# Hybrid decoder block on one core: the store of the rotary queries split over two stages, and the third stage's second scores set ahead of its gating matmuls

## The chip, the core and the metric

The kernel runs on one core of a Trainium2 chip. The metric is the device time of one execution in microseconds (us); lower is better. Inputs and output are float32 arrays in DRAM and are part of the measured program. TensorE (PE in the profile) does the matrix products, VectorE (DVE), ScalarE (ACT) and GpSimd (POOL) do the element work, and SyncE (SP) issues every DMA, in one queue and in a fixed order.

## The reference

One decoder layer of width 1024 over 528 positions (16 learned meta tokens ahead of 512 real ones). One projection feeds two attention branches of 16 heads each, MLA (latent queries and keys with a rotary part of 32) and FoX (a forget gate in the logits), both gated and merged:

```python
u = rmsnorm(h, pre_norm_g[l])
proj = u @ w_in[l]
(cq, ckv, k_pe_raw, z_mla, fq, fk, fv, f_logit, z_fox, gate_a, gate_b) = jnp.split(proj, split_idx, axis=-1)
...
q_m = jnp.concatenate([q_nope, rope(q_pe, pos)], axis=-1)
k_m = jnp.concatenate([k_nope, jnp.broadcast_to(k_pe, (B, MLA_HEADS, L, MLA_ROPE_DIM))], axis=-1)
o_mla = causal_block_attention(q_m, k_m, v_mla, MLA_SCALE)
y_mla = (o_mla * jax.nn.silu(z_mla)) @ w_br_mla[l]
...
o_fox = causal_block_attention(fox_heads(fq), fox_heads(fk), fox_heads(fv), FOX_SCALE, cum)
y_fox = (o_fox * jax.nn.silu(z_fox)) @ w_br_fox[l]
mixed = (jax.nn.sigmoid(gate_a) * y_mla + jax.nn.sigmoid(gate_b) * y_fox) @ w_out[l]
h = h + rmsnorm(mixed, post_norm_g[l])
```

The four query blocks of 128 positions see the meta tokens and the causal keys. The output leaves the meta tokens out.

## The kernel before, in words

Every product in float32 precision is made of three matmuls on a high and a low part of both operands (`wh`, `wl` of weights, `uTh`, `uTl` of the normed input). Weights arrive by DMA as `wraw` (512 KB for a block of 128 columns); ACT casts the high part (`wh`, line 130 or 604) and POOL or DVE subtracts to get the low part (`wl`, line 103).

After a first part (norms, small projections) the attention runs in 16 stages. The list `stages` has, for each of eight pairs of heads, FoX (`br` = 1) and then MLA (`br` = 0); the loop's counter `si` is 0 for the first stage. So the second stage is MLA of pair 0, the third FoX of pair 1, the fourth MLA of pair 1. In the loop, PE's order is written out by hand, as the kernel's functions are called:

- `s0()` and `s1()` are the scores: matmuls into `st`, then for each query block DVE's masked pass with the row minimum (`sf`, `nb`, line 789) and ACT's exponential (line 797). `s0` covers query blocks 0 to 2, `s1` block 3.
- `n0()` and `n1()` norm them: DVE takes reciprocals of the row sums (`su`, `ri`, lines 805 and 806), POOL does the meta columns, ACT writes the high half of the probabilities (`pn`, line 824) and DVE the low half (line 825). A DMA transpose for each of eight (block, head) pairs then turns `pn` into `pt`, one `pt` for each of the two heads.
- `va()` of a stage is its values step: matmuls `ov` of `vp` (the values, turned by a DMA transpose of `vh`) and `pt`; then DVE's gated result `gT` (line 845). It is called in the next stage, after that one's `s0`. So the third stage's PE order holds the second stage's `ov`.
- `fill` is the list of projection steps that stand between these: of a FoX stage the two gating products `z` (24 matmuls each for both branches of this pair), and the next stage's queries `mq`, keys `mk` and values `v`; of an MLA stage the next FoX stage's `fq`, `fk`, `v`. `early` says how many of its steps go between `s0` and `va`.

```python
early = {0: 3, 2: 4, 9: 4}.get(si, 0)
s0()
run(fill[:early])
for fn in late:
    fn()
s1()
```

Projection results share three PSUM buffers (`accp`), so the fourth product in a row waits until the first has been read: in the third stage `mk` waits for the reader of `z`, which is DVE's `sil` (line 738) after ACT's tanh (line 737). The instructions of DVE, ACT, POOL and SP are put in order by the framework's scheduler; PE alone follows the order of the calls, and SP where `written[0]` is set (below).

The rotary part of MLA's queries is computed before the stages for heads 0 to 7 (`pe_unit(0)`): its halves lie in rows 4 and 5 of `gT0` and `gT1`, 16 partitions for a head. Heads 0 and 1 go straight into `QP`; the six others are stored to `qpe_dram` and read back as `QP`, two heads at a time, for pairs 1 to 3. The store is four DMAs, one for each half `x` and part `i`; it is called with a range of heads:

```python
def store(x, a, b):
    for i in range(2):
        dma(qpe_dram[8 * g + a : 8 * g + b, i, x], results(x)[16 * a : 16 * b, i])
```

While `written[0]` is set, a DMA keeps its place in the order of the program on SP's queue.

Of the kernel before, what the change touches and what calls it, by code (L numbers as in the profile page):

```python
# [54 lines left out]
def block_kernel(ctx: ExitStack, tc: tile.TileContext, x, meta_tokens, pre_norm_g, w_in, fox_forget_b,  # L55
# [29 lines left out]
    written, sums_out = [False], []  # L85
# [135 lines left out]
    def run(steps):  # L221
        for _, fn in steps:
            fn()
# [324 lines left out]
    def gate_unit():  # L548

        i, br = gates.pop(0)  # L550

        def done(_, ps):
            ths[i, br] = thp.tile([128, S], F32, tag="th", name=f"th{i}{br}")
            nc.scalar.activation(ths[i, br], ps, AF.Tanh, scale=0.5)
        return unit(f"pg{i}{br}", win_w((O_GA, O_GB)[br], i), u_act, KD, REAL, done)


    with ExitStack() as att:
# [294 lines left out]

        stages = [(br, pr) for pr in range(NH // 2) for br in (1, 0)]

        vts = {}

        def feed(br, pr):
# [12 lines left out]
        pe0, rest0, store0 = pe_unit(0)  # L871
# [5 lines left out]
        for si, (br, pr) in enumerate(stages):  # L877
# [3 lines left out]
            if br == 1:  # L881

                za, zb = z_unit(1, pr), z_unit(0, pr)
                fill = (vts[br, pr] if pr else begun) + za + q + zb[:3] + k + zb[3:5] + v + zb[5:]
            elif not last:

                fill = vts[br, pr] + q + k[:KD] + v + k[KD:]
            else:
                g = gate_unit()
                fill = vts[br, pr] + g + gate_unit() + gate_unit()  # L890
# [20 lines left out]
        for si, (br, pr) in enumerate(stages):  # L911
            s0, s1, n0, n1, va = attention(br, pr)

            fill = fills[si]
            early = {0: 3, 2: 4, 9: 4}.get(si, 0)
            s0()
            run(fill[:early])
            for fn in late:
                fn()
            s1()  # L920

            if si == 0:

                run(fill[early:5])
                run(vts[1, 0] + pe_rest)
                n0()
                low[0] = nc.vector
                for ahead_ in [fn.prep for _, fn in fill[5:] if hasattr(fn, "prep")][:2]:
                    ahead_()
                low[0] = nc.gpsimd  # L930
                n1()
                first_t.extend(through)
                run(fill[5:])
            else:
                if si == 1:

                    written[0] = True
                    for x in range(2):
                        store0(x, 2, 8)
                    written[0] = False  # L940
                run(fill[early:5])
                if si == 1:

                    behind[:] = exps[:1]
                if si == 2:
                    behind.clear()
                n0()
                run(fill[5:11])
                if br:

                    behind[:] = [halved[("k", 1, pr), 1]]
                run(fill[11:12])
                if br:
                    behind.clear()
                n1()
                if 6 <= si < 8:

                    written[0] = True
                    rest1(si - 6)
                    written[0] = False  # L960
                run(fill[12:])
            written[0] = False
            if si == 1:

                behind[:] = [halved[("k", 1, 1), 0]]
            late = [va]
# [232 lines left out]
```

## Time and profile before

| what | value |
|---|---|
| median of 3 runs | 607.18 us (605.46 to 607.64) |
| profiled execution, its own time | 606.9 us |
| its span in the profile | 605.1 us |
| PE busy | 593.5 us, 98% of the span |
| second stage on PE (from its first `st`) | 80.0 to 103.2 us |
| third stage | 103.2 to 127.7 us |
| fourth stage | 127.7 to 150.7 us |

Times in a view are microseconds from the start of the span. A timeline row has start, duration, engine, line, operation, tiles, shape and count, and in brackets the idle time of the engine just before it with what ended it. "SPq" rows are DMA issues: their duration is that of the issue, not of the transfer. Matmul rows overlap by their pipeline: from start to start is the pace. PEclk is the clock that TensorE was granted, 1.00 being full.

### The profile page before, as it was taken

What the parts mean: (1) busy time and instruction counts of PE and PEld (TensorE: products, weight loads), DVE (VectorE), ACT (ScalarE), POOL (GpSimd) and SP (SyncE); (2) the same over time, 40 slices, a digit from 0 to 9 for tenths busy, and PEclk for the clock granted to TensorE, in tenths of its full rate; (3) what the DMA queues carried; (4) which work ended last, traced back from release to release, by engine and by line L of the source; (5) the groups of instructions that cost most, each with busy time, mean ns of one, the idle gap of its engine ahead of it and who ended that gap; (6) DMA issues with size and microseconds to landing.
All of it is one profiled execution on the core that took longest, in us unless ns stands there. A gap on an engine that the chain in (4) does not pass through costs nothing.

```text
span 605.1 us, 11002 instructions
## 1 busy us (share of the span) xinstructions
PE 593.5 (98%) x3777; PEld 502.9 (83%) x3777; DVE 375.2 (62%) x1004; ACT 342.4 (57%) x786; POOL 179.5 (30%) x239
## 2 busy tenths in 40 slices
PE   8999999899999999999999999999999999999996
PEld 6889889679889889889888898887888888888884
DVE  6946776564774774675766657773733624367857
ACT  7846773764773774675766748761221433243653
POOL 4317543353437544345433534530000000000000
PEclk9999999989999999999999999999999999999999
DMA  8533798988698698979797985988534323332603
GB/s 288 120 86 95 122 186 195 211 168 192 120 195 164 145 210 161 197 169 203 128 179 173 160 187 140 199 168 260 192 105 104 99 79 102 104 98 89 233 0 140
DMA packets 219960, 93.25 MB, mean 154 GB/s; under 512 B 133420, under 2 KB 211636, under 8 KB 219904
## 3 DMA queue, kind: packets, MB, share of 16 engines
q1 hardware_dynamic: 219904, 92.55, 66.3%
q8 instruction: 30, 0.49, 0.3%
q14 instruction: 26, 0.21, 0.1%
HBM read 58.10 MB, written 4.00 MB: 103 GB/s over the span
## 4 chain that ended last, share of the span: by engine, by line
PE 79%; ACT 1%; DVE 0%; issue 0%; DVEq 0%; ACTq 0%
PE py L97 14%; PE z L97 14%; PE pg L97 14%; PE st L97 7%; PE v L97 7%; PE fk L97 6%; PE fq L97 6%; PE ov L97 5%; PE x L97 4%; PE mq L97 1%; PE mk L97 1%; PE y L97 1%; PE ppe L97 0%; ACT wh L130 0%; DVE yo L1107 0%
## 5 line engine op out<-in xcount | busy, mean ns | idle before, releaser
L103 POOL TENSOR_TENSOR wl<-wraw,wh 128x1024 fp32r<-128x1024 f32 (+2 forms) x62 | 119.7, 1939 | 106.8 <-ACT wh L130 80.2
L130 ACT CAST wh<-wraw 128x1024 fp32r<-128x1024 f32 (+1 forms) x80 | 83.1, 1042 | 119.4 <-PE pg L97 38.5
L797 ACT ACTIVATE sf<-sf,nb 128x144 f32<-128x144 f32 (+3 forms) x128 | 72.0, 564 | 12.3 <-DVE nb L789 11.8
L825 DVE SCALAR_TENSOR_TENSOR pn<-sf,ri,pn 128x128 f16<-128x128 f32 (+3 forms) x128 | 69.1, 578 | 13.6 <-ACT pn L824 12.7
L824 ACT ACTIVATE pn<-sf,ri 128x128 f16<-128x128 f32 (+3 forms) x128 | 61.5, 551 | 19.5 <-ACT sf L797 16.8
L103 DVE TENSOR_TENSOR wl<-wraw,wh 128x1024 fp32r<-128x1024 f32 x34 | 41.6, 1222 | 42.8 <-ACT wh L130 42.8
L97 PE MATMUL z<-uTh,wh 128*128 128x512 f32 x128 | 51.5, 402 | 0.0
L789 DVE CUSTOM_DVE_ANT_0 sf<-st,maskt 128x272 f32<-128x272 f32 (+2 forms) x128 | 48.6, 435 | 3.9 <-PE st L97 3.9
L97 PE MATMUL z<-uTl,wh 128*128 128x512 f32 x128 | 50.5, 395 | 0.0
L97 PE MATMUL z<-uTh,wl 128*128 128x512 f32 x128 | 50.4, 394 | 0.0
L97 PE MATMUL pg<-uTh,wh 128*128 128x512 f32 x128 | 50.3, 393 | 0.0
L97 PE MATMUL pg<-uTl,wh 128*128 128x512 f32 x128 | 49.8, 389 | 0.0
L97 PE MATMUL pg<-uTh,wl 128*128 128x512 f32 x128 | 49.8, 389 | 0.0
L97 PE MATMUL py<-gh,wh 128*128 128x512 f32 x128 | 49.8, 389 | 0.0
L97 PE MATMUL py<-gl,wh 128*128 128x512 f32 x128 | 49.8, 389 | 0.0
L97 PE MATMUL py<-gh,wl 128*128 128x512 f32 x128 | 49.8, 389 | 0.0
L97 PE MATMUL st<-hlk,hlq 64*128 64x272 f32 (+3 forms) x480 | 47.3, 306 | 0.0
L97 PEld LDWEIGHTS st<-hlk,hlq 64*128 64x128 f32 x480 | 35.0, 185 | 5.8 <-ACT vh L721 2.8
L702 DVE TENSOR_REDUCE vsc<-v 128x1 f32<-128x272 f32 (+1 forms) x32 | 13.2, 432 | 38.8 <-PE v L97 38.8
L97 PE MATMUL v<-uTh,wl 128*128 128x256 f32 (+1 forms) x128 | 36.5, 285 | 0.0
L97 PE MATMUL fk<-uTl,wh 128*128 128x256 f32 (+1 forms) x128 | 36.4, 285 | 0.0
L97 PE MATMUL fk<-uTh,wh 128*128 128x256 f32 (+1 forms) x128 | 36.4, 285 | 0.0
(233 smaller groups left out, 1434.1 us busy)
## 6 DMA issues: line engine op xcount, KB each, us to landing
wraw<-in_w_in_dram SPq DMA_DIRECT2D x56, 512.0 KB
wraw<-in_w_br_fox_dram SPq DMA_DIRECT2D x8, 512.0 KB
tb<-in_w_out_dram SPq DMA_DIRECT2D x8, 512.0 KB
wraw<-in_w_br_mla_dram SPq DMA_DIRECT2D x8, 512.0 KB
wraw<-in_w_out_dram SPq DMA_DIRECT2D x6, 512.0 KB
pt<-pn SPq DMA_TRANSPOSE x128
xr<-in_x_dram SPq DMA_DIRECT2D x4, 512.0 KB
out_dram<-yo SPq DMA_DIRECT2D x8, 256.0 KB
```

Of the source, the lines that this page charges most:

```text
L97: nc.tensor.matmul(*a, **k)
L103: return eng.tensor_tensor(out=lo, in0=src, in1=f32(hi), op=ALU.subtract)
L130: nc.scalar.copy(wh[:, :n], raw[:, :n])
L702: nc.vector.tensor_reduce(out=sc[:, i : i + 1], in_=ps, op=ALU.max, axis=AX.X, apply_absolute_value=True)
L789: nc.vector.tensor_tensor_reduce(out=sf_of(h, b)[:, c0 : c0 + w], in0=ps[h][:, o : o + w], in1=maskt[:, m0 : m0 + w], scale=-scale, scalar ...
L797: exps[g] = nc.scalar.activation(sf, sf, AF.Exp, bias=sums["nb"][:, h, b : b + 1], scale=-1.0, accum_out=sums["su"][:, h, b : b + 1]).ins
L824: nc.scalar.activation(hi, sf, AF.Copy, scale=rib)
L825: nc.vector.scalar_tensor_tensor(out=lo, in0=sf, scalar=rib, in1=hi, op0=ALU.mult, op1=ALU.subtract)
```

## The change

There are two edits, both in the loop over the stages. The first makes the store in two parts: heads 2 and 3 in the second stage, where all six were stored, and heads 4 to 7 in the fourth stage, after three steps of its `fill`. Each part is four DMAs. The second takes the entry of the third stage out of `early`: no step of `fill` stands between its `s0` and the second stage's `va` any more; the first four entries of the list (the DMA transpose of the values, which issues nothing on PE, and three steps of the FoX `z` product, nine matmuls) come after `s1` instead.

```diff
+        def stores(a, b):
+
+            written[0] = True
+            for x in range(2):
+                store0(x, a, b)
+            written[0] = False
+
...
-            early = {0: 3, 2: 4, 9: 4}.get(si, 0)
+            early = {0: 3, 9: 4}.get(si, 0)
...
                 if si == 1:
 
-                    written[0] = True
-                    for x in range(2):
-                        store0(x, 2, 8)
-                    written[0] = False
-                run(fill[early:5])
+                    stores(2, 4)
+                run(fill[early:3])
+                if si == 3:
+                    stores(4, 8)
+                run(fill[max(early, 3):5])
                 if si == 1:
```

The order on the engines shows what this moves. On SP in the second stage, the four stores (`qpe_dram`, a minus for before, a plus for after) stand between the loads of two weights and the transpose of the values:

```order
 L91 DMA wraw_1052<-in_w_in_dram 128x8x128
 L91 DMA wraw_1064<-in_w_in_dram 128x8x128
-L91 DMA qpe_dram<-gT_778 6x16x512 x2
-L91 DMA qpe_dram<-gT_779 6x16x512 x2
+L91 DMA qpe_dram<-gT_778 2x16x512 x2
+L91 DMA qpe_dram<-gT_779 2x16x512 x2
 L91 DMA_TRANSPOSE vp_729<-vh 128x9x128
 L91 DMA CT<-c_dram 2x528
```

Their place and number stay; each has two heads of 16 rows in place of six.

On PE in the third stage, before: the last `st` matmuls of `s0`, then nine of `z`, of which the first rows are shown, and then `ov`.

```order
634 L97 MATMUL st_1475<-CT,ONE 128x400
635 L97 MATMUL st_1476<-CT,ONE 128x400
636 L97 MATMUL z_1500<-uTh,wh_1494 128x512
637 L97 MATMUL z_1500<-uTl,wh_1494 128x512
638 L97 MATMUL z_1500<-uTh,wl_1495 128x512
```

At the same place after:

```order
634 L97 MATMUL st_1475<-CT,ONE 128x400
635 L97 MATMUL st_1476<-CT,ONE 128x400
636 L97 LDWEIGHTS vp_729
637 L97 MATMUL ov_1493<-pt_726,vp_729 64x512
638 L97 LDWEIGHTS vp_729
639 L97 MATMUL ov_1493<-pt_727,vp_729 64x512
```

The second stage's `ov` now follows directly on `s0`, and the 24 matmuls of `z` stand in one piece after `s1`.

On DVE in the third stage, before: the low halves of the probabilities `pn`, with the gated result `gT` of the second stage behind four of them, and then `s1`'s masked passes (`sf_1538`).

```order
L805 TENSOR_SCALAR su_1450<-su_1450 128x2x3
L806 RECIPROCAL ri_1451<-su_1450 128x2x3
L825 SCALAR_TENSOR_TENSOR pn_724<-sf_1452,ri_1451,pn_724 128x128 x2
L825 SCALAR_TENSOR_TENSOR pn_724<-sf_1452,ri_1451,pn_724 128x2x128 x2
L845 SCALAR_TENSOR_TENSOR gT_778<-ov_1510,vsc_1099,sil_1126 128x512
L825 SCALAR_TENSOR_TENSOR pn_724<-sf_1452,ri_1451,pn_724 128x3x128
L789 ISA sf_1538,nb_1449<-st_1539,maskt 128x272
```

After:

```order
L805 TENSOR_SCALAR su_1450<-su_1450 128x2x3
L806 RECIPROCAL ri_1451<-su_1450 128x2x3
L845 SCALAR_TENSOR_TENSOR gT_778<-ov_1493,vsc_1099,sil_1126 128x512
L825 SCALAR_TENSOR_TENSOR pn_724<-sf_1452,ri_1451,pn_724 128x128
L789 ISA sf_1521,nb_1449<-st_1522,maskt 128x272
```

`gT` stands ahead of all the low halves, and `s1`'s first masked pass behind one of them in place of five. On ACT, in the same stage, the cast of the fourth stage's `fq` weights (`wh_1819`) and the tanh of `z` change places: the cast is first now.

On SP in the fourth stage, before: after the last load of a weight come the weights of `mq` and the transpose of the values.

```order
L91 DMA wraw_1823<-in_w_in_dram 128x8x128
L91 DMA wraw_1882<-in_w_uq_dram 128x2x192
L91 DMA wraw_1882<-in_w_ukv_dram 128x256
L91 DMA_TRANSPOSE vp_729<-vh 128x9x128
L91 DMA wraw_1930<-in_w_in_dram 128x8x128
```

After:

```order
L91 DMA wraw_1823<-in_w_in_dram 128x8x128
L91 DMA qpe_dram<-gT_778 4x16x512 x2
L91 DMA qpe_dram<-gT_779 4x16x512 x2
L91 DMA wraw_1886<-in_w_uq_dram 128x2x192
L91 DMA wraw_1886<-in_w_ukv_dram 128x256
L91 DMA_TRANSPOSE vp_729<-vh 128x9x128
L91 DMA wraw_1934<-in_w_in_dram 128x8x128
```

Four DMAs of four heads each are added there, ahead of five others.

## The prediction

> **What bounds the kernel now.** I read the page's head first, then the chain that ended last, then PE's waits, and then the one stage in which these lie.
>
> ```profile
> span 605.1 us, 11002 instructions
> PE 593.5 (98%) x3777; PEld 502.9 (83%) x3777; DVE 375.2 (62%) x1004; ACT 342.4 (57%) x786; POOL 179.5 (30%) x239
> ```
>
> PE is the bound, with 11.6 us of idle time in the whole span. PE's waits name what can be won around the change:
>
> ```profile
> PE mk L97 <- DVE sil L738: 1.5, 1, 1.5
> ...
> PE ov L97 <- DMA pt<-pn: 0.6, 1, 0.6
> PE mk L97 <- DVE hlq L103: 0.6, 1, 0.6
> ```
>
> All three lie in the third stage. The table by stretches shows them, and the granted clock behind them:
>
> ```profile
> core 0: us, PE busy (x) PEld busy (x) DVE busy (x) ACT busy (x) POOL busy (x), PEclk, DMA share, GB/s
> ...
> 105.21:108.50 3.29, 2.67 (x11) 1.75 (x12) 1.65 (x10) 2.20 (x7) 1.07 (x1) 1.00 1.15 248
> 108.50:111.61 3.11, 3.11 (x42) 2.54 (x41) 0.63 (x3) 2.60 (x11) 1.86 (x4) 1.00 1.13 330
> ...
> 118.60:121.70 3.10, 1.06 (x6) 0.70 (x6) 2.60 (x5) 2.43 (x5) 1.47 (x1) 1.00 0.47 89
> 121.70:125.10 3.40, 3.40 (x12) 2.81 (x12) 0.49 (x2) 0.37 (x1) 0.90 (x1) 0.50 0.92 174
> ```
>
> The first wait costs 0.62 (3.29 - 2.67), the two others 2.04 (3.10 - 1.06), and right after these PE runs 3.40 us at clock 0.50, which loses another 1.7. PE's own rows:
>
> ```profile
> 104.86 0.35 PE L97 MATMUL st<-CT,ONE 64*128 64x400 f32 x2
> ...
> 107.54 0.38 PE L97 MATMUL ov<-pt,vp 80*64 80x512 f16 x1
> 108.50 2.01 PE L97 MATMUL ov<-pt,vp 80*64 80x512 f16 x25 [0.58 <-DMA pt<-pn]
> ...
> 111.61 0.50 PE L97 MATMUL z<-uTh,wh 128*128 128x512 f32 x1
> ...
> 118.36 0.39 PE L97 MATMUL z<-uTh,wl 128*128 128x512 f32 x1
> 120.23 0.39 PE L97 MATMUL mk<-cTh,wh 128*128 128x272 f32 x1 [1.48 <-DVE sil L738]
> ...
> 122.04 0.63 PE L97 MATMUL z<-uTh,wh 128*128 128x512 f32 x1
> ```
>
> Between `s0`'s end (104.86 + 0.35 = 105.21) and the first `ov` (107.54) stand the nine `z` matmuls that the change takes away from there. The second `ov` needs the other head's `pt`, which landed at 108.50.
>
> **The store, split.** The queue that decides when `pt` lands:
>
> ```profile
> 62.61 4.96 SPq L91 DMA_DIRECT2D QP<-gT  x8
> ...
> 81.65 4.21 SPq L91 DMA_DIRECT2D qpe_dram<-gT  x4
> 85.97 4.09 SPq L91 DMA_TRANSPOSE vp<-vh  x1
> ```
> ```profile
> 105.11 1.35 SPq L91 DMA_TRANSPOSE pt<-pn  x1
> ```
> ```profile
> 86.00:88.40 2.40, 2.40 (x11) 1.99 (x12) 2.39 (x8) 2.40 (x8) 2.34 (x4) 1.00 0.40 148
> 239.45:239.95 0.50, 0.50 (x8) 0.34 (x4) 0.42 (x3) 0.22 (x2) 0.27 (x1) 1.00 0.56 187
> ```
>
> The second stage's last transpose was issued until 106.46 and landed 2.04 later; the one before it, issued until 105.11, then landed at about 107.15, and no later than 107.54. The last two rows are stretches in which stores alone ran: the six heads of the second stage (DMA share 0.40, 148 GB/s) and eight heads of a later store (0.56, 187 GB/s). Six of 16 engines are 0.38, eight are 0.50, and both move 23 to 25 GB/s per head. So a store seems to run on as many DMA engines as it has heads, each with the same bytes. The four stores before are 786 KB, 5.3 us at 148 GB/s.
>
> What two heads take, no row of before shows. One bound: a third of the bytes at the same 148 GB/s, 1.8 us. The other: two engines at 24.7 GB/s each, 262 KB at 49 GB/s, 5.3 us again. I take the second, since both rows go by heads; then `vp` and all transposes behind it on these engines land as before.
>
> [...]
>
> **`z` behind `s1`.** PE reaches `ov` at 105.21 and waits for the same landings: idle from 105.21 to 108.50 but for one `ov` (0.38), that is 2.9 in place of 0.62. From 108.50 `ov` and `s1` go as before to 111.61. Then come 24 `z` in a row, for whose pace there is a row of the chain:
>
> ```profile
> 155.81 5.65 PE z L97 x24
> ```
>
> So nine more take 2.12. Before, 15 `z`, six `mq` and nine `z` took 111.61 to 118.75 (118.36 + 0.39), 7.14; now PE is ready for `mk` at 111.61 + 7.14 + 2.12 = 120.87. The work moved fills the second wait, if `sil` is there by then. DVE, then ACT, before:
>
> ```profile
> 110.63 0.19 DVE L806 RECIPROCAL ri<-su 128x6 f32<-128x6 f32 x1
> ...
> 112.88 0.74 DVE L845 SCALAR_TENSOR_TENSOR gT<-ov,vsc,sil 128x512 f32<-128x512 f32 x1
> ...
> 114.07 0.43 DVE L789 CUSTOM_DVE_ANT_0 sf<-st,maskt 128x272 f32<-128x272 f32 x1
> ...
> 115.60 0.60 DVE L825 SCALAR_TENSOR_TENSOR pn<-sf,ri,pn 128x384 f16<-128x384 f32 x1
> ...
> 119.49 0.68 DVE L738 SCALAR_TENSOR_TENSOR sil<-sil,z 128x512 f32<-128x512 f32 x1
> ```
> ```profile
> 106.30 1.05 ACT L130 CAST wh<-wraw 128x1024 fp32r<-128x1024 f32 x1 [2.58 <-DMA wraw<-in_w_in_dram]
> ...
> 115.36 0.74 ACT L797 ACTIVATE sf<-sf,nb 128x528 f32<-128x528 f32 x1 [1.96 <-DVE nb L789]
> ...
> 117.40 1.34 ACT L824 ACTIVATE pn<-sf,ri 128x512 f16<-128x512 f32 x2 [0.49 <-ACT sf L797]
> 118.65 0.57 ACT L737 ACTIVATE sil<-z 128x512 f32<-128x512 f32 x1
> 119.12 1.03 ACT L130 CAST wh<-wraw 128x1024 fp32r<-128x1024 f32 x1
> ```
>
> After: `gT` follows the reciprocal (110.82 to 111.56; `ov` ends at 110.51), one low half (0.4), two masked passes (0.72), one low half, two passes (0.81): `s1`'s four passes (114.07 to 115.60 before, with `gT` and five low halves ahead) end at 113.9, 1.7 earlier, and ACT's exponentials (115.36) start 1.6 earlier. DVE has four low halves left, 2.0 us, to 115.9; with 0.36 for sums and reciprocals ACT's last two `pn` go at 116.4 in place of 117.40 and end at 117.65. The cast now stands ahead of the tanh and needs the last `z` (111.61 + 5.65 = 117.3): to 118.7, tanh to 119.2, `sil` to 119.9. That is 1.0 before PE's 120.87. No wait, and `hlq`, 0.7 of DVE behind `sil`, is in time for the second `mk`. Six `mk` at 0.12 take 0.75, so the next `z` starts at 121.6 in place of 122.04: a gain of 0.4.
>
> **The clock.** The 1.7 for the half clock would be won if PE's idle time no longer caused it. But 2.04 idle of 3.10 brought it before, and now 2.9 of 3.29 are idle in one place. I take it that the slow stretch only moves, to `ov`, `s1` and the first `z`, and count nothing for it; the other bound is a gain of 1.7. The three runs (605.46, 607.18, 607.64) differ by that much, so by my estimate the fastest had no slow stretch.
>
> [...]
>
> **The store's other part, in the fourth stage.**
>
> ```profile
> 124.89 0.55 SPq L91 DMA_DIRECT2D wraw<-in_w_in_dram  x1
> 129.23 0.40 SPq L91 DMA_DIRECT2D wraw<-in_w_uq_dram  x1
> ...
> 130.23 1.45 SPq L91 DMA_TRANSPOSE vp<-vh  x1
> ...
> 134.70 2.48 SPq L91 DMA_TRANSPOSE pt<-pn  x2
> ...
> 139.81 6.88 SPq L91 DMA_TRANSPOSE pt<-pn  x5
> ```
> ```profile
> 152.60 0.84 PE L97 MATMUL ov<-pt,vp 80*64 80x512 f16 x6
> ```
>
> Four more issues go between 125.44 and 129.23, where SP issued nothing for 3.8 us. By the second stage's rows they take 4.2, and `vp` behind them 2.6 more (4.09 against 1.45): 6.8. SP's two pauses, 3.8 and the 2.2 ahead of 134.70 (waiting for `pn`), take 6.0. The rest, 0.8, moves this stage's transposes: the last, issued to 146.69 and landing 2.04 later at 148.7, would land at 149.5, 3.1 ahead of its reader at 152.60. The `QP` load of heads 4 and 5, issued at about 137.3, has the stores behind it by some 134. I cost this at nothing; without that cover it is at most the 6.8 less the 3.9 of slack at 152.60, 2.9.
>
> **The sum.** +2.3 first wait, -2.0 second, -0.7 for fewer breaks in PE's stream (`z` in one piece, `mk` without stops; this is what is left between the waits and the 0.4), clock 0, fourth stage 0: -0.4. From the profiled execution's 606.9: 606.5. The median of the runs is 0.3 above that execution, 607.18: 606.8 there.
>
> **Rivals.**
> - Bytes decide, not heads. SP's four issues shrink to 2.5 (0.62 each, as `QP<-gT` at 62.61), `vp` to 1.45 or little more: 3.7 to 4.3 earlier, so `pt` lands by 104.8, before 105.21. `ov` then starts at once, and `s1` ends at 108.7 in place of 111.61; ACT's cast at 106.30, which waited for a load of the same queue, comes earlier too. Gain 0.4 + 2.9 + 1.7 = 5.0: 602.2 on the median. Against it: the shares 0.40 and 0.56.
> - The clock stays full: 606.8 - 1.7 = 605.1. It hangs on where the idle time falls.
> - Slower: the second wait stays beside the first. DVE's `gT` now stands ahead of all low halves and waits for `ov`; if `ov` and what hangs on it comes over 1.0 later than I have it while PE does not, `mk` waits again. At the old 2.04 that gives 608.8, with a second slow stretch 610.5.
> - The fourth stage pays: 607.18 + 2.5 = 609.7.
>
> **How the numbers follow.** Forecast (landings as before) 0.64, of which 0.20 with full clock; bytes decide, wholly or in part, 0.18; second wait stays 0.13; fourth stage 0.05. The likeliest alone runs from 604.8 to 607.4. The range reaches into the first and third rivals, 603.0 to 609.6, and leaves about 0.2 out. Some 0.5% (3 us) is what a measurement here can tell from no change: below 604.1 is most of the byte rival, 0.17; above 610.2 the worst of the two slow ones, 0.08.
>
> **What would show it.** PE's wait for `pt` ahead of `ov` near 2.9 in place of 0.6, and no wait of `mk`; in the second stage a DMA share near 0.13 while the stores run, for some 5 us; `vp`'s issue there still near 4; a stretch of clock 0.50 starting about 108 to 112 in place of 121.70; the fourth stage's `ov` without a wait. I am wrong if the wait for `pt` stays under 1, or if `mk` still waits for `sil`.

## The result and the profile after

The changed kernel takes 607.51 us (median of 14 runs, 605.50 to 608.93), the kernel before, measured beside it, 607.15 (14 runs, 604.08 to 609.20). The ratio is 1.0009, 95% interval 0.9992 to 1.0027: no difference that can be told. The forecast was 606.8 and "same". On the other chips of the experiments below the kernel before took 604.6 to 606.1, so times are set against the kernel before beside them.

The profiled execution of the changed kernel took 607.82, 0.92 more than the one before (606.9). The head of its page, and PE's waits (in all, times, longest):

```profile
span 606.0 us, 11003 instructions
PE 593.9 (98%) x3777; PEld 505.1 (83%) x3777; DVE 375.1 (62%) x1004; ACT 342.7 (57%) x786; POOL 179.4 (30%) x239
```
```profile
PE ov L97 <- issue: 3.2, 1, 3.2
...
PE ov L97 <- DMA pt<-pn: 0.4, 1, 0.4
```

Both waits of `mk` are gone. In their place stands one ahead of `ov`, 3.2 + 0.4 = 3.6 us. (The page puts its larger part down to "issue", but it ends with the landing of the first `pt`, as the second does with that of the other: in the trace's DMA records the four-byte writes that close the two transposes end at 107.71 and 108.74, and each `ov` starts 0.5 later. In the kernel before they end at 106.97 and 108.00, with the same 0.5 to its second `ov`.) PE's rows, and the place where `mk` waited:

```profile
104.73 0.34 PE L97 MATMUL st<-CT,ONE 64*128 64x400 f32 x2
108.25 0.61 PE L97 MATMUL ov<-pt,vp 80*64 80x512 f16 x1 [3.18 <-issue]
109.22 3.79 PE L97 MATMUL ov<-pt,vp 80*64 80x512 f16 x25 [0.37 <-DMA pt<-pn]
...
114.51 0.50 PE L97 MATMUL z<-uTh,wh 128*128 128x512 f32 x1
...
123.33 0.39 PE L97 MATMUL z<-uTh,wl 128*128 128x512 f32 x1
123.56 0.29 PE L97 MATMUL mk<-cTh,wh 128*128 128x272 f32 x1
```
```profile
113.05 0.75 DVE L845 SCALAR_TENSOR_TENSOR gT<-ov,vsc,sil 128x512 f32<-128x512 f32 x1 [1.51 <-PE ov L97]
...
121.68 0.69 DVE L738 SCALAR_TENSOR_TENSOR sil<-sil,z 128x512 f32<-128x512 f32 x1 [1.15 <-ACT sil L737]
```

`sil` ends at 122.37, 1.2 ahead of `mk`. The 25 `ov` from 109.22 take 3.79 where they took 2.01 before. The table by stretches says why in its last two rows; the row ahead of them shows the second stage's stores:

```profile
core 0: us, PE busy (x) PEld busy (x) DVE busy (x) ACT busy (x) POOL busy (x), PEclk, DMA share, GB/s
...
88.40:91.20 2.80, 2.80 (x14) 2.32 (x13) 2.80 (x6) 2.04 (x5) 2.70 (x2) 1.00 0.15 48
...
107.02:113.85 6.83, 5.23 (x34) 3.76 (x36) 1.16 (x4) 6.31 (x19) 3.50 (x5) 0.50 1.16 279
103.61:107.02 3.41, 1.46 (x20) 1.12 (x18) 2.68 (x13) 0.00 (x0) 0.00 (x0) 1.00 0.99 205
```

The clock is 0.50 for 6.83 us, twice the 3.40 of before, and it starts in the wait itself. SP's issues in the second and in the fourth stage, and PE's rows of the fourth stage's `ov` and of the reader of that stage's `pt`:

```profile
81.40 2.98 SPq L91 DMA_DIRECT2D qpe_dram<-gT  x4
84.49 3.89 SPq L91 DMA_TRANSPOSE vp<-vh  x1
...
89.46 2.52 SPq L91 DMA_DIRECT2D CT<-c_dram  x1
...
126.74 2.84 SPq L91 DMA_DIRECT2D qpe_dram<-gT  x4
...
132.03 1.64 SPq L91 DMA_TRANSPOSE vp<-vh  x1
...
141.50 6.83 SPq L91 DMA_TRANSPOSE pt<-pn  x5
```
```profile
130.87 0.62 PE L97 MATMUL ov<-pt,vp 80*64 80x512 f16 x4
...
153.49 0.84 PE L97 MATMUL ov<-pt,vp 80*64 80x512 f16 x6
```

Two heads move 48 GB/s at a share of 0.15, and `vp` behind them still takes 3.89 to issue. The DMA records show the count itself: the store's packets have 2048 bytes, and at a time 6 of them (the median) were under way with six heads, 2 with two heads, 4 with the four heads of the fourth stage. The 384 packets of before ran from 85.32 to 91.52, the 128 of now from 85.52 to 91.17. Neither `ov` has a wait; the first of them started at 129.98 in the kernel before.

### The profile page after: what moved, and what is told of

Same layout as the page of the kernel before. It is cut to its first block, busy times and chain, and to the rows that moved or that the text cites. A ratio compares the mean times of both kernels' runs of the same rounds, so it can differ in the third digit from the quotient of the medians.

```text
span 606.0 us, 11003 instructions
## 1 busy us (share of the span) xinstructions
PE 593.9 (98%) x3777; PEld 505.1 (83%) x3777; DVE 375.1 (62%) x1004; ACT 342.7 (57%) x786; POOL 179.4 (30%) x239
## 4 chain that ended last, share of the span: by engine, by line
PE 96%; ACT 2%; DMA 1%; DVE 1%; issue 0%; DVEq 0%; ACTq 0%
PE z L97 17%; PE pg L97 15%; PE py L97 14%; PE st L97 9%; PE v L97 9%; PE fk L97 8%; PE fq L97 7%; PE ov L97 6%; PE x L97 4%; PE psm L97 3%; PE mq L97 2%; PE mk L97 1%; PE ppe L97 1%; PE spun L97 1%; PE y L97 1%; DMA pt<-pn 1%
## 5 line engine op out<-in xcount | busy, mean ns | idle before, releaser
L97 PE MATMUL ov<-pt,vp 128*64 128x512 f16 (+4 forms) x416 | 35.2, 318 | 3.5 <-issue 3.2
L97 PEld LDWEIGHTS <-vp 128*64 128x64 f16 (+1 forms) x416 | 24.0, 113 | 16.5 <-issue 9.0
```

Of the source, the lines that this page charges most:

```text
L97: nc.tensor.matmul(*a, **k)
```

## The experiments

All ratios are to the kernel before, run on the same chip, with 95% intervals; they are not the quotients of the two medians shown. Line numbers in rows of these kernels can be one to three higher than those of the kernel above.

| kernel | median | before beside it | ratio |
|---|---|---|---|
| split of the store alone | 606.11 | 605.53 | 1.0020 (1.0000 to 1.0039) |
| third stage's order alone | 605.10 | 605.53 | 0.9998 (0.9980 to 1.0016) |
| before, wide store | 602.95 | 605.53 | 0.9964 (0.9950 to 0.9979) |
| changed, wide store | 602.75 | 605.53 | 0.9972 (0.9955 to 0.9988) |
| changed, wide store, a second time | 601.48 | 604.61 | 0.9945 (0.9923 to 0.9967) |
| changed, wait filled | 606.42 | 605.04 | 1.0025 (1.0010 to 1.0041) |
| changed, a second time | 606.27 | 606.07 | 1.0000 (0.9980 to 1.0020) |
| changed, wait filled, DVE's order held | 605.84 | 606.07 | 1.0011 (0.9992 to 1.0029) |
| before, wide store and order | 601.37 | 606.07 | 0.9928 (0.9910 to 0.9946) |
| changed, no late store | 605.72 | 604.61 | 1.0016 (0.9997 to 1.0036) |
| changed, wide store, no late store | 601.29 | 604.61 | 0.9942 (0.9919 to 0.9964) |

**Each edit alone.** The split, with the nine `z` ahead of `ov`:

```diff
-            early = {0: 3, 9: 4}.get(si, 0)
+            early = {0: 3, 2: 4, 9: 4}.get(si, 0)
```

> The first edit alone: the store in two parts, the third stage's order as in the kernel before (nine z ahead of ov). My theory (a store runs on as many engines as it has heads, so two heads take as long as six): pt lands as before, the wait ahead of the third stage's ov is about 0.6 us, mk waits 1.5 and 0.6 us, clock 0.50 for 3.4 us behind it, the fourth stage without a wait: 606.7 to 607.7. Rival, bytes decide: the transposes land some 4 us earlier, no wait ahead of ov, 602 to 603. Rival, the four stores of the fourth stage cost time of their own: ov of that stage waits, 608 to 610.

The order, with one store of six heads (to the kernel before):

```diff
-            early = {0: 3, 2: 4, 9: 4}.get(si, 0)
+            early = {0: 3, 9: 4}.get(si, 0)
```

> The second edit alone: one store of six heads, and no z ahead of the third stage's ov. If this edit carries all that the changed kernel's trace shows in the third stage: wait ahead of ov 2.9 to 3.6 us, no wait of mk, clock 0.50 for 3.4 to 6.8 us around ov and s1, 606.8 to 608. If the smaller store had shortened that wait (bytes), this kernel would be slower than the changed one by up to 4 us, about 611. If the half clock for 6.8 us came from the split store and not from the order, 3.4 us of it and about 606.

The split gives no time (the rival "bytes decide" is out: 606.11, not 602 to 603), and its interval reaches from nothing to 2.4 us lost. Its fourth stage has no wait. The order alone is within 1.2 us of the kernel before either way. Both medians lie below what I had expected (606.7 to 607.7 and 606.8 to 608), but so does the kernel before beside them, with 605.53 in place of 607.15. Here is `ov` in the two traces, first with the split alone and then with the order alone:

```profile
106.67 0.39 PE L97 MATMUL z<-uTh,wl 128*128 128x512 f32 x1
108.19 0.38 PE L97 MATMUL ov<-pt,vp 80*64 80x512 f16 x1 [1.13 <-issue]
109.16 2.94 PE L97 MATMUL ov<-pt,vp 80*64 80x512 f16 x25 [0.59 <-DMA pt<-pn]
```
```profile
105.34 0.36 PE L97 MATMUL st<-CT,ONE 64*128 64x400 f32 x2
107.78 0.38 PE L97 MATMUL ov<-pt,vp 80*64 80x512 f16 x1 [2.08 <-issue]
108.74 3.66 PE L97 MATMUL ov<-pt,vp 80*64 80x512 f16 x25 [0.58 <-DMA pt<-pn]
```

With the order alone the wait is 2.66, 0.24 below the lower end expected, and `mk` has none. Both have one stretch of clock 0.50, of 3.41 us, right at `ov`: the 25 `ov` take 2.94 and 3.66, where they took 2.01 in the kernel before. With the split alone that is not where I expected it: there the clock fell after waits of 1.13 and 0.59, not behind `mk`, whose first wait was gone (its second still stood, 0.6). I had also written that 3.41 us of half clock with the order alone would put the 6.83 down to the split store. That does not follow: the changed kernel itself had 6.83 in its first trace and none in its second (below), so the length belongs to the execution.

**The wide store.** If heads set the number of engines, as the 2, 4 and 6 packets under way suggest, a store whose heads and rows are one dimension of 96 should, by my estimate from these, use all 16. The target's layout changes, and the read back of a pair becomes two loads:

```diff
-    qpe_dram = dram.tile([NH, 2, 2, 16, S], F32, tag="qpedram", name="qpe_dram")
+    qpe_dram = dram.tile([2, 2, NH, 16, S], F32, tag="qpedram", name="qpe_dram")
...
-            dma(f32(QP), qpe_dram[2 * pr : 2 * pr + 2].rearrange("h i x f s -> (h i x f) s"))
+            for h in range(2):
+                dma(f32(QP[64 * h : 64 * h + 64]), qpe_dram[:, :, 2 * pr + h].rearrange("i x f s -> (i x) f s"))
...
-                    dma(qpe_dram[8 * g + a : 8 * g + b, i, x], results(x)[16 * a : 16 * b, i])
+                    dma(qpe_dram[i, x, 8 * g + a : 8 * g + b].rearrange("h f s -> (h f) s"), results(x)[16 * a : 16 * b, i])
```

On the kernel before:

> The kernel before with the store's target in DRAM laid out so that the heads and their 16 rows are one dimension of 96 (the same bytes, four stores; the read back becomes two loads of 64 rows each). If the number of engines of a store is set by its slowest dimension, these run on 16 in place of 6 and take about 2.2 us in place of 5.3: the issue of vp falls from 4.1 to 1.5 to 2 us, the last pt of the second stage lands about 2 us earlier (near 106.5 in place of 108.5), no wait ahead of ov, of mk at most 0.4, no stretch of clock 0.50: 603 to 604.5. If the stores' engines are not what holds vp back (SP's own issues, or the bytes), 606.7 to 607.7.

```profile
80.90 2.91 SPq L91 DMA_DIRECT2D qpe_dram<-gT  x4
83.91 1.68 SPq L91 DMA_TRANSPOSE vp<-vh  x1
...
98.57 3.42 SPq L91 DMA_TRANSPOSE pt<-pn  x2
```
```profile
84.50:87.30 2.80, 2.80 (x26) 2.36 (x25) 2.21 (x8) 2.80 (x8) 1.73 (x5) 1.00 1.13 326
```
```profile
106.70 0.39 PE L97 MATMUL z<-uTh,wl 128*128 128x512 f32 x1
107.02 2.04 PE L97 MATMUL ov<-pt,vp 80*64 80x512 f16 x26
...
117.56 0.40 PE L97 MATMUL mk<-cTh,wh 128*128 128x272 f32 x1 [0.23 <-DVE sil L739]
...
118.76 0.38 PE L97 MATMUL mk<-cTh,wh 128*128 128x256 f32 x1 [0.55 <-DVE hlq L103]
```

The same 384 packets now run from 84.43 to 87.07, 2.64 us in place of 6.20, with 16 under way at a time (the median). The 326 GB/s of the window, against 148 before, are not the store's alone, but 369 of the window's 1025 packets, and 0.76 of its 0.91 MB, are. `vp`'s issue falls from 4.09 to 1.68, and the second stage's last transposes are issued by 101.99 in place of 106.46. That is 4.5 earlier, where I had expected 2: 2.1 of it is that SP reaches `vp` sooner (0.75 because the stores' issue began sooner in this execution, 1.3 because it was shorter), and 2.4 that `vp` no longer waits behind the stores. No wait of `ov`, no stretch of clock 0.50 in the stages (mean clock 0.998), 602.95 us, just under the 603 to 604.5 expected. So the packets under way were 2 with two heads (a share of 0.15, 48 GB/s), 4 with four, 6 with six, and 16 with one dimension of 96.

On the changed kernel, the same edit:

> The changed kernel with the same layout of the store's target, so that two heads are one dimension of 32 and four heads one of 64. Engines theory: 16 engines in place of 2, the four stores take under 1 us, pt lands 2 to 3 us earlier (105.6 to 106.6), the wait ahead of ov falls from 3.6 to 0.4 to 1.4, no wait of mk, clock 1.00 throughout or one stretch of 3.4 us: 603 to 605. If something else sets the landing (SP's issues): wait unchanged, 607 to 608.

No wait of `ov` or `mk` is left in its trace, where I had expected 0.4 to 1.4, and the clock is full until the program's end (mean 0.999); 602.75 us, just under the 603 to 605 expected, spread from 601.39 to 605.57.

**The wait, filled.** Does PE's idle time bring the half clock, and what is that worth?

```diff
+                if (br, pr) == (0, 0):
+                    for _ in range(13):
+                        mm(po, ONE, uTh[:, 0, META:L], start=True, stop=True)
                 for h in range(2):
                     mm(ph[h], vps[br][0:80, 0, 64 * h : 64 * h + 64], pts[h][0:80, 0], start=True, stop=False)
```

> The changed kernel with 13 more matmuls of no use (about 3 us, into the tile that ov overwrites) between s0 and ov in the third stage, where PE waits for pt. The wait is as long as before but PE is busy in it. If PE's idle time brings the half clock: no stretch of clock 0.50 near 107 to 114, and 604 to 605.8 (3.4 us of full speed won, or 1.7 if one of the two windows stays). If the half clock has another cause, or if it costs nothing there: 607 to 608.

In all 12 executions the mean clock was 0.997 or more, against 2 of the 14 of the changed kernel, which ran on another chip: with the idle time filled the clock stayed up. (The next run has the two side by side.) But 606.42 us were 0.6 above the upper end that I had expected for a gain, on a chip where the kernel before took 605.04. The trace had a second cause in it. The scheduler had moved `gT` on DVE behind all six low halves:

```profile
112.23 2.74 DVE L825 SCALAR_TENSOR_TENSOR pn<-sf,ri,pn 128x128 f16<-128x128 f32 x6 [0.52 <-ACT pn L824]
114.89 0.74 DVE L848 SCALAR_TENSOR_TENSOR gT<-ov,vsc,sil 128x512 f32<-128x512 f32 x1
115.55 0.43 DVE L789 CUSTOM_DVE_ANT_0 sf<-st,maskt 128x272 f32<-128x272 f32 x1
```

`s1`'s first masked pass started at 115.55 although `s1`'s matmuls were done 2.0 earlier than in the changed kernel, so `sil` came no earlier and `mk` waited 0.75 again. The next kernel holds DVE to the changed kernel's order (each low half of that stage is put behind the step that it follows there); in the traces all engines then have the changed kernel's order but for the 13 matmuls. Beside it ran the changed kernel itself.

```diff
+                            last = (steps[0, 0] if n == 0 else steps[1, 1, 1][1 if n == 1 else 3]) if (br, pr, g) == (1, 1, 0) else None
+                            with tc.issue_after(last) if (br, pr, g) == (1, 1, 0) else nullcontext():
```

> The changed kernel with 13 matmuls of no use ahead of the third stage's ov, as in the run before, and this time with DVE held to the changed kernel's order in that stage (in the run before, gT had slipped behind all six low halves, s1's masked passes came 1.3 us later, and mk waited 0.75 us for sil). Theory, the half clock's price is hidden only in part: clock 1.00 throughout, s1 ends 2.0 us earlier, and sil comes 1.0 to 1.5 us earlier with it, so mk waits 0.3 us or less and 1.5 to 2.3 us are won against the changed kernel. Rival, something else holds sil at 122 (ACT's cast, the load behind it): mk waits 0.7 us or more again, and no more than 1 us is won.

> The changed kernel itself, on the same chip as the two kernels beside it, so that they can be set against it. Its own trace: pt lands as late as in its first profile, clock 0.50 for 3.4 or 6.8 us around ov: 1.0 to 3 us over the kernel before where that runs at full clock, 0.4 to 0.7 over it where that has its slow stretch.

The filled kernel's trace does what the theory says; `mk` has no wait:

```profile
108.15 2.04 PE L98 MATMUL ov<-pt,vp 80*64 80x512 f16 x26
```
```profile
118.46 0.69 DVE L739 SCALAR_TENSOR_TENSOR sil<-sil,z 128x512 f32<-128x512 f32 x1 [1.03 <-ACT sil L738]
```
```profile
120.11 0.39 PE L98 MATMUL z<-uTh,wl 128*128 128x512 f32 x1
120.34 0.29 PE L98 MATMUL mk<-cTh,wh 128*128 128x272 f32 x1
```

Its mean clock was 0.997 or more in 11 of 12 executions, against 6 of 12 of the changed kernel beside it. The time does not follow: 605.84 against 606.27 is 0.4 less, but the ratios, 1.0011 and 1.0000, point the other way, and the intervals overlap. Of the 1.5 to 2.3 us expected nothing can be told. Two things may explain a part, and the rest stays open. On that chip half of the changed kernel's executions (6 of 12) had a mean clock of 0.997 or more anyway, so only half of the price could be won; and in the filled kernel `ov` cannot start before the 13 matmuls end, while in the changed kernel's trace here the second `pt` was there 1 us earlier than in the first:

```profile
107.29 0.38 PE L97 MATMUL ov<-pt,vp 80*64 80x512 f16 x1 [1.54 <-issue]
108.26 1.95 PE L97 MATMUL ov<-pt,vp 80*64 80x512 f16 x24 [0.59 <-DMA pt<-pn]
```

Within the traces the price does show. From the third stage's first `st` to the fourth stage's `ov` the changed kernel took 27.75 in its first trace (half clock for 6.83), 23.93 in this one (full clock), and the filled kernel 24.58: 3.2 less than the one and 0.65 more than the other. But this second trace, with the shorter third stage, is of an execution of 606.66 us, and the filled kernel's of one of 604.63: the time was lost outside the third stage, where this trace has more waits (0.88 and 0.32 ahead of later `ov`, 0.8 in the part ahead of the stages).

What the half clock costs in the whole time is better read from the kernel before. Over the four chips of these experiments it was executed 92 times: 40 with a mean clock of 0.996 or less (median 606.4), 52 with more (median 604.3), so about 2 us (1.5 to 2.5 by chip). That is a comparison of executions, not of kernels, and the mean clock is a rough sign: it also holds the half clock at the program's end, from 602.95 in the trace of the kernel before and from 601.96 in the changed kernel's.

**Order and wide store together,** six heads stored in the second stage (the wide kernel before, less the entry `2: 4` of `early`):

> The kernel before with the wide store (all six heads in the second stage, on 16 engines) and the second edit: no z ahead of the third stage's ov. pt lands at about 104.0, before s0 ends at 104.8 to 105.0. If the order is worth something once pt is in time, mk's two waits of the wide kernel (0.23 and 0.55 us) go and nothing takes their place: 0.5 to 1 us less than the wide kernel, 601.8 to 602.5. If only the landing of pt mattered: the same as the wide kernel, 602.9. If the split store had a worth of its own beside the width: more than 0.5 us slower than the changed kernel with the wide store (602.75).

```profile
105.04 0.36 PE L97 MATMUL st<-CT,ONE 64*128 64x400 f32 x2
105.33 2.04 PE L97 MATMUL ov<-pt,vp 80*64 80x512 f16 x26
...
117.27 0.39 PE L97 MATMUL z<-uTh,wl 128*128 128x512 f32 x1
117.50 0.29 PE L97 MATMUL mk<-cTh,wh 128*128 128x272 f32 x1
```

No wait at all in the third stage, 601.37 us: faster than both kernels (0.9928 of the kernel before, 4.4 us), a little below what I had expected, and 1.6 less than the wide store without the order, on intervals that don't touch (0.9910 to 0.9946, 0.9950 to 0.9979). These two ran on different chips; there the kernel before, where its mean clock was above 0.996, took 604.25 and 604.32, so the chips differ by less than that. In the traces, from the first `ov` of the program (82.71, in the other 82.14) to the fourth stage's (124.88, 125.79) it is 42.17 in place of 43.65, 1.48 less: `mk`'s two waits, 0.78, and 0.70 that is left over, which I put down to fewer breaks. The three other traces with the wide store and the order (two of the changed kernel with it, one without late stores) agree: from the third stage's first `st` to the fourth stage's `ov` all four take 21.41 to 21.43, the wide store without the order 22.92. So the order that is worth nothing in the change is worth 1.5 us in that stretch once `pt` is in time. In whole times it is less sure: on one chip, the changed kernel with the wide store, which has the order too, was only 0.2 under the wide store without it (602.75 and 602.95), with 6 of its 12 executions at 603.3 or more; what slowed these is not shown. A second time, on another chip, the same kernel took 601.48 (below).

**The fourth stage's stores.** The wide changed kernel had come out at 0.9972, well above 0.9928, and the changed kernel's second trace showed a wait in the fifth stage that the first did not have:

```profile
151.64 2.04 PE L97 MATMUL ov<-pt,vp 80*64 80x512 f16 x25 [0.88 <-DMA pt<-pn]
```

So the four late stores were taken out, with pairs 2 and 3 reading heads 2 and 3 in place of their own, and the wide changed kernel ran again beside.

```diff
         def load_qp(pr):
+            pr = 1 if pr in (2, 3) else pr
...
-                if si == 3:
-                    stores(4, 8)
```

> The changed kernel without the four stores of the fourth stage (the rotary queries of heads 4 to 7 are left out; pairs 2 and 3 read those of heads 2 and 3 in their place). All else stands as in the changed kernel. If those stores are hidden, as I predicted, the same as the changed kernel: 1.000 to 1.001 of the kernel before. If they cost time where the third stage runs at full clock (a trace of the changed kernel showed waits of 0.88 and 0.32 us for pt in the fifth and sixth stage): 1 us less, 0.997 to 0.999, and a narrower spread.

> The changed kernel with the wide store, and without the four stores of the fourth stage (heads 4 to 7 left out as in the run beside it). With them it took 0.9972 of the kernel before, and six heads stored in the second stage took 0.9928. If the fourth stage's stores are what costs the difference: 0.992 to 0.993 and a spread of about 1 us, as there. If it is the rest of the split (two heads in place of six in the second stage, other landings): 0.996 to 0.998.

> The changed kernel with the wide store again, now on one chip with the two kernels beside it, since it is the difference to it that counts: 0.996 to 0.998 of the kernel before, with a spread of 3 to 4 us. If it comes out at 0.993 here, the difference between it and the kernel with six heads in the second stage was one between chips, and the fourth stage's stores cost nothing.

Without the late stores: 1.0016 and 0.9942; with them 1.0000 to 1.0009 and, on the same chip, 0.9945 (601.48 against 601.29). They cost nothing that can be measured. My guess that they were behind the 0.9972 was wrong; that ratio was one of its chip or its executions, which is not settled, and the wide store is as good split as whole (0.9945 and 0.9928, overlapping intervals). The 0.88 is real in that execution, but not the rule. (The second trace of the changed kernel with the wide store has 0.71 ahead of the sixth stage's `ov`, in an execution of 602.55.)

## Why the prediction was right, and where it was not

The forecast of no change held, the time lies within the range, and most of the mechanisms were as described; in the sum two terms were too small, and both make the kernel slower. Against the profiled execution before, -0.4 was forecast and +0.9 came. By itself the number proves little: "same" would have come of the full-clock rival and of the second wait too, and the two executions compared are single ones of kernels whose runs spread over 3.4 and 5.1 us. What bears the mechanism out are the signs named ahead, and the split and the wide store on their own.

- *The store runs on as many engines as it has heads:* right. 0.15 and 48 GB/s where 0.13 and 49 were forecast, 2 packets under way at a time, `vp`'s issue 3.89 ("near 4"), and the split alone wins nothing. The first rival (602.2) is out. The wide store turns the same claim round: 16 packets under way, and `pt` in time.
- *`pt` lands as before:* in the first profile it did not; the second `ov` started at 109.22 in place of 108.50, so the wait became 3.55 in place of 2.9. Part of that may lie on SP: the second `CT`, which took 0.37 to issue before, now took 2.52 behind the two-head stores, and the last two transposes are issued from 103.23 in place of 102.90 and take 3.95 in place of 3.56. But it is no larger than the scatter: in the changed kernel's second trace that `ov` starts at 108.26. I took a landing in one profile for a fixed time.
- *The second wait goes, with `sil` 1.0 ahead of `mk`:* right, 1.2 ahead. `mk` (123.56 in place of 120.87) and `sil` (122.37 in place of 119.9) both came later, by 2.7 and 2.5.
- *0.7 from fewer breaks:* not contradicted. The forecast had it as what was left between other terms; in the pair of wide kernels 0.70 is again what is left. No run measures it by itself.
- *The clock, counted 0:* this is the term that was mis-sized. The stretch did move to the wait, as the prediction said, and started 1.0 ahead of the 108 to 112 named there, at 107.02; but it was 6.83 us in place of 3.40. PE was busy for 5.23 of it, which loses 2.6 in place of 1.7: +0.9. The sum then closes: 3.55 - 0.62 = +2.9, second wait -2.0, breaks -0.7, clock +0.9 make +1.1; the fourth stage's `ov` starts at 130.87 in place of 129.98, with a third stage that began 0.14 earlier: +1.0.
- *Full clock as a rival (605.1):* it happens, in 2 of the first 14 executions (605.50 and 605.71) and in 6 of 12 on another chip (four of these took 603.4 to 604.2, two 606.2 and 606.7), as it does in the kernel before (52 of 92). It is no property of the change.
- *Second wait stays (608.8):* not in the changed kernel. It came back at 0.75 where the filled kernel's DVE order put `gT` late: that is close to the mechanism that I had named, the masked passes late and PE in time, but there `gT` stood behind six low halves and did not wait for `ov`.
- *The fourth stage hides its stores:* right, though by another sum. The issue of the four stores took 2.84, not 4.2, `vp`'s issue grew to 1.64, not 4.09, and taking the stores out gains nothing.

## What to carry to other kernels

Look at the shape of a DMA before its size: with a slowest dimension of 6 these stores had 6 packets under way and took 6.20 us, and a third of the bytes, with a slowest dimension of 2 and 2 packets under way, took 5.65; with heads and rows as one dimension of 96 it was 16 under way and 2.64 us. That layout won 2.2 us (0.9964) where the whole change won nothing. An order that fills one engine's wait pays only if what it moves forward is ready: here 1.5 us were there to be won, and went into a wait for a transfer, until the transfer came earlier. And a wait can cost more than its own length: here idle time of 1.7 to 3.6 us, in two pieces each time, was followed by the lower clock (0.50, for 3.41 or 6.83 us), so sum the idle time by stretches and not by instructions.

## What was not expected of the hardware

In the traces of the two kernels the lower clock came on a grid. In the kernel before it lasted 3.413 us in the third stage and began 116.05 us after the trace's first clock entry (at 5.62), and once more, at the program's end, 597.33 after it: 34 and 175 times 3.413. In the changed kernel it lasted 6.827, twice that, and began 98.99 after the first entry (at 8.04), and at the program's end 593.92 after it: 29 and 174 times. So the 3.41 us right ahead of each drop can be looked at. Four such rows, of the kernel before, the split alone, the order alone and the changed kernel without late stores, and one where no drop followed, of the changed kernel's second trace:

```profile
118.26:121.67 3.41, 1.37 (x8) 0.73 (x7) 2.91 (x5) 2.77 (x5) 1.51 (x2) 1.00 0.54 102
```
```profile
106.65:110.06 3.41, 1.68 (x13) 0.82 (x13) 0.00 (x0) 3.08 (x10) 1.96 (x1) 1.00 1.11 240
```
```profile
105.30:108.72 3.42, 0.78 (x7) 0.27 (x4) 2.06 (x12) 2.17 (x6) 1.04 (x1) 1.00 1.17 259
```
```profile
104.29:107.71 3.42, 0.75 (x9) 0.42 (x6) 2.25 (x12) 1.37 (x4) 0.24 (x1) 1.00 1.21 254
```
```profile
106.07:109.49 3.42, 1.61 (x15) 1.10 (x17) 1.34 (x6) 3.42 (x12) 2.30 (x1) 1.00 1.13 265
```

The changed kernel's is above (103.61:107.02, PE busy 1.46). The clock fell after windows with PE busy for 0.75, 0.78, 1.37, 1.46 and 1.68 of 3.41, and did not after 1.61. Over all whole windows of the grid with the full clock in the traces of the two kernels (those at the program's end too), it fell after the four with PE busy for 1.46 or less, and after none of the others, which had 2.79 or more. The 6.83 fit too: the first half of it had PE busy for 1.82, and the clock stayed low. So by my estimate from these windows the border lies near one half, within what modelled ends of matmuls can say. Two waits of some 2 us came out differently: 1.48 + 0.55 in the kernel before was followed by the half clock, 1.54 + 0.59 in the changed kernel's second trace was not; of the 3.41 us of their rows PE was idle for 2.04 in the first and 1.81 in the second. That the place of the wait on the grid decides this is an estimate from these two, and no run sets it.
